# Seven block products of a feed-forward's second matmul in another order, and activation sums, chunks and loads that follow it

## The chip, the cores and the metric

The kernel runs on one core of a Trainium2 chip. The metric is the device time of one execution in microseconds, the median of three runs where nothing else is said. The engines are named as the profile names them: PE (TensorE, matrix products), DVE (VectorE), ACT (ScalarE), POOL (GpSimd) and SP (SyncE, which here issues the loads and stores).

## The reference

A block of two layers works on 1024 latent tokens and 256 context tokens of 1024 features, all in float32. Each layer normalises its input (RMS norm with a scale and a shift made from a conditioning vector), mixes the tokens by attention, adds a gated residual, normalises again and runs a feed-forward; the first layer's attention looks at a neighbourhood of a grid, the second one's at all tokens, with normalised queries and keys. Cut to what matters here:

```python
h_lat = ada_norm(x, g, shift, scale)
x = x + gate1 * mixer(h_lat, h_ctx)
h = ada_norm(x, g2, shift2, scale2)
a, g = split(h @ w_in, 2)           # 1024 -> 2 * 2816
x = x + gate2 * ((silu(g) * a) @ w_out)   # 2816 -> 1024
```

The context's tokens go through the same steps in layer 0 only, and after layer 1 a last norm with a scale and a shift gives the output.

## The kernel before, in words

Every product of float32 numbers is made of three products of shorter words: an operand is split into a high word (a cast, on ACT) and a low word (operand minus high word, `combine` on DVE, L951, or POOL, L948), and PE multiplies high by high, high by low and low by high. So each weight and each activation costs one cast and one subtraction beside its matmuls.

The two feed-forwards (`class Ffn`, one object for each layer) use seven block products in place of eight. The latent tokens form two blocks of 512 (block 0 and block 1), and `PARTS` names the products P1 to P7: each has a weight, plain (W11, W12, W22) or a sum (S1 to S4), and an activation, plain (A11, A21, A22) or a sum (T1 to T4). In the first matmul (`mm1`, L1443 to L1445) the outer loop runs over `NJ` = 22 chunks of 128 hidden features, and each chunk goes through its products. The first `fill` chunks do only P1 and P2 at first (in layer 0 with the context's part, C22 and C21); the rest of their products follows in a second pass. `load1` loads each chunk's raw weights into the cells of the stock `raws`, `feed1` starts an `operand` for each split (L1419), `sums` makes the activation sums T1 to T4 for each quarter k. In the second matmul (`mm2`, L1684 to L1686) the outer loop runs over the products in the order of `ORDER2`; each takes four PSUM banks and 11 steps of three matmuls into each bank, 132 matmuls. `load_t` and `load_w` load its activations and weights, `feed2`, `weight2` and `value2` split them. `drain` then empties the banks: it adds a bank to the residual rows of those quadrants that `SUMS2` names (`add`, L1726), and one partial product, U2, is kept in SBUF, completed by a second product and added to three quadrants from there, 12 additions of 128x512. `load_c` loads the residual rows that these additions go to. In layer 0 the context's second matmul follows (`ctx2`, L1339 to L1341, four quarters), fed by `feed_ctx`. At its start, `load_h` loads the first block's residual rows for the norm, and `ctx_norm` the context's.

`norm` (L121) squares eight rows of a block on ACT (L156), adds them on DVE and POOL (L144), lets PE sum over the partitions (L189) and takes the root on ACT; `apply_norm` scales the rows and splits them (L210, L134, L198, L131, L132). After the first feed-forward `norms1` runs it for both blocks for layer 1, whose key and value projections come next; after the second one `finals` and `output` run the last norm and store the result.

The order on every engine is fixed beforehand: `Lanes` (`bg`) is a planner that runs all these generators against modelled costs, in three lines of priority (`bg.enter(tag, generator, delay, line)`, line 0 first), and writes each instruction to the program where its generator gets the engine. On the chip each engine then goes through its list strictly in order, and waits where an operand isn't there. A changed delay, line or order therefore moves instructions of all engines.

## Time and profile before

| | us |
|---|---|
| median of 3 runs (lowest, highest) | 3114.68 (3112.24, 3115.24) |
| the profiled execution's own time | 3110.32 |
| its span from first to last instruction | 3108.5 |
| PE busy | 2941.1 (95%) |
| DVE busy | 2321.2 (75%) |
| POOL busy | 1800.0 (58%) |
| ACT busy | 1619.0 (52%) |
| chain of work that ended last, by engine | PE 68%, DVE 10%, POOL 6%, DMA 6% |

The mean granted clock of TensorE is 0.985 of full speed. The first feed-forward lies between about 750 and 1700 us, the second from about 2380 to the end; the attention of layer 1 lies between them. The profile is one execution, the median is over three others.

### The profile page before, as it was taken

Reading aid. Unit: us, or ns where it says so; the run is one execution under the profiler, and the core shown is the slowest. Engines: PE = TensorE matmul, PEld = TensorE weight load, DVE = VectorE, ACT = ScalarE, POOL = GpSimd, SP = SyncE. Lnnn points to the kernel's source line nnn. Section 1 sums busy time; section 2 is a strip of 40 time slices with the busy share of each in tenths; the row PEclk is TensorE's granted clock in tenths of the full one; section 3 lists DMA queues with packets and bytes.
Section 4 is the critical chain, followed back from the end, with each engine's and each line's share of the span. In section 5 each row is a group of like instructions: output and inputs, shape, how many; then the busy total and the mean of one; then the engine's idle time right before and its main releaser. Section 6 shows DMA issues by size and latency. Waiting matters only on the chain.

```text
span 3108.5 us, 50198 instructions
## 1 busy us (share of the span) xinstructions
PE 2941.1 (95%) x16460; PEld 2512.9 (81%) x16460; DVE 2321.2 (75%) x4287; ACT 1619.0 (52%) x3735; POOL 1800.0 (58%) x1484
## 2 busy tenths in 40 slices
PE   7999998998899999999988899999999899999997
PEld 4898997887688888887868778888887678888885
DVE  7488778775887677556797588899897786666668
ACT  4345546775642322234455488898886623333444
POOL 4246556765675454346786156666644685445676
PEclk9999999999999999999999999999999999999999
DMA  7777767787335554258455523333323343234862
GB/s 260 216 239 235 231 216 224 235 229 219 132 122 178 169 180 159 77 200 288 164 181 195 166 83 99 98 102 106 106 76 119 125 142 105 102 108 166 314 196 87
DMA packets 306019, 516.94 MB, mean 166 GB/s; under 512 B 46304, under 2 KB 111968, under 8 KB 303968
## 3 DMA queue, kind: packets, MB, share of 16 engines
q1 hardware_dynamic: 305760, 513.74, 51.1%
q8 instruction: 131, 2.15, 0.3%
q14 instruction: 128, 1.05, 0.1%
HBM read 387.52 MB, written 120.18 MB: 163 GB/s over the span
## 4 chain that ended last, share of the span: by engine, by line
PE 68%; DVE 10%; POOL 6%; DMA 6%; issue 4%; ACT 4%; SPq 1%; DVEq 0%; POOLq 0%; ACTq 0%
PE pf L1445 9%; PE pf L1443 9%; PE pf L1444 9%; PE T L863 5%; PE o L494 5%; PE ps L766 3%; PE ps L767 3%; PE ps L768 3%; PE pf L1686 2%; PE pf L1685 2%; PE pf L1684 2%; PE S L2220 2%; PE S L2221 2%; POOL c L948 1%; DMA K<-Kd 1%
## 5 line engine op out<-in xcount | busy, mean ns | idle before, releaser
L856 POOL TENSOR_SCALAR Pt<-Pt,rc 128x1280 f32<-128x1280 f32 (+3 forms) x288 | 298.4, 1036 | 391.5 <-ACT pT L871 139.6
L871 ACT CAST pT<-T 128x256 fp32r<-128x256 f32 (+2 forms) x672 | 304.8, 477 | 122.8 <-PE T L863 118.4
L876 DVE TENSOR_TENSOR pT<-T,pT 128x256 fp32r<-128x256 f32 (+2 forms) x672 | 342.1, 535 | 31.3 <-ACT pT L871 30.9
L863 PE MATMUL T<-ident,Pt 128*128 128x128 f32 x1952 | 303.2, 275 | 22.6 <-POOL Pt L856 22.0
L863 PEld LDWEIGHTS T<-ident,Pt 128*128 128x128 f32 x1952 | 235.5, 141 | 78.6 <-POOL Pt L856 34.7
L494 PE MATMUL o<-pT,Vt 128*128 128x256 f32 x1952 | 296.0, 290 | 2.3 <-DVE pT L876 2.2
L766 PE MATMUL ps<-ah,wh 128*128 128x512 f32 (+1 forms) x688 | 261.2, 380 | 5.2 <-ACT ah L429 2.3
L494 PEld LDWEIGHTS o<-pT,Vt 128*128 128x128 f32 x1952 | 254.8, 189 | 9.5 <-DVE pT L876 5.6
L767 PE MATMUL ps<-al,wh 128*128 128x512 f32 (+1 forms) x688 | 251.3, 365 | 5.3 <-POOL al L132 3.6
L768 PE MATMUL ps<-ah,wl 128*128 128x512 f32 (+1 forms) x688 | 251.0, 365 | 1.4 <-DVE wl L335 1.4
L845 ACT ACTIVATE Pt<-S,rc 128x512 f32<-128x512 f32 (+2 forms) x384 | 247.2, 654 | 9.7 <-DVE rc L837 6.2
L948 POOL TENSOR_TENSOR c<-c,c 128x512 fp32r<-128x512 f32 (+1 forms) x104 | 152.7, 1471 | 125.9 <-ACT c L1419 85.9
L1445 PE MATMUL pf<-ah,wl 128*128 128x512 f32 x480 | 190.4, 397 | 17.6 <-DVE wl L951 15.6
L2212 DVE TENSOR_REDUCE nm<-S 128x1 f32<-128x512 f32 x256 | 169.7, 683 | 35.3 <-PE S L2221 33.6
L1443 PE MATMUL pf<-ah,wh 128*128 128x512 f32 x480 | 190.0, 396 | 2.2 <-ACT wh L1419 2.2
L1444 PE MATMUL pf<-al,wh 128*128 128x512 f32 x480 | 189.4, 395 | 0.0
L891 POOL TENSOR_TENSOR r<-ob 128x256 f32<-128x256 f32 x144 | 123.5, 857 | 65.2 <-ACT ob L885 59.1
L845 ACT ACTIVATE Pt<-X,rc 128x256 f32<-128x256 f32 x256 | 125.1, 489 | 64.9 <-DVE rc L837 58.1
L1419 ACT CAST wh<-c 128x512 fp32r<-128x512 f32 x111 | 68.7, 620 | 169.1 <-POOL c L948 60.1
L768 PEld LDWEIGHTS ps<-ah,wl 128*128 128x128 f32 x688 | 130.9, 190 | 23.2 <-DVE wl L335 2.1
L767 PEld LDWEIGHTS ps<-al,wh 128*128 128x128 f32 x688 | 131.9, 192 | 18.4 <-POOL al L132 5.3
L766 PEld LDWEIGHTS ps<-ah,wh 128*128 128x128 f32 x688 | 131.5, 191 | 18.3 <-ACT ah L429 2.5
(598 smaller groups left out, 9530.5 us busy)
## 6 DMA issues: line engine op xcount, KB each, us to landing
wr<-in_wqkv SPq DMA_DIRECT2D x53, 512.0 KB, 4.5
rope<-in_fout SPq DMA_DIRECT2D x98, 256.0 KB, 3.8
wr<-in_adaT SPq DMA_DIRECT2D x96, 256.0 KB, 3.0
c<-in_fout SPq DMA_DIRECT2D x77, 256.0 KB, 3.5
rope<-in_fin SPq DMA_DIRECT2D x69, 256.0 KB, 3.0
adaw<-in_adaT SPq DMA_DIRECT2D x64, 256.0 KB, 3.7
wr<-in_wo SPq DMA_DIRECT2D x32, 512.0 KB, 4.0
K<-Kd SPq DMA_DIRECT2D x64, 224.0 KB, 4.4
```

Of the source, the lines that this page charges most:

```text
L494: t.matmul(o_ap, lhsT=u.V[:, kb, :], rhs=u.pT[:, i, :], start=i == 0, stop=i == len(u.blocks) - 1)
L766: t.matmul(ps, lhsT=hi[:, c], rhs=ah[:, kc, :n], start=kc == 0, stop=False)
L767: t.matmul(ps, lhsT=hi[:, c], rhs=al[:, kc, :n], start=False, stop=False)
L768: t.matmul(ps, lhsT=lo[:, c], rhs=ah[:, kc, :n], start=False, stop=kc == KC - 1)
L845: s.activation(u.Pt[:, off:off + u.wid[c]], u.S[c], AF.Exp, bias=u.min, scale=u.sign, accum_out=u.rc[:, 3 + c:4 + c])
L856: g.tensor_scalar(Pt, Pt, u.rc[:, 2:3], 1.0, ALU.mult, ALU.mult)
L863: t.transpose(T[:, i * P:(i + 1) * P], u.Pt[:, (i0 + i) * P:(i0 + i + 1) * P], ident[:])
L871: s.copy(u.pT[:, i0:i0 + n, :P], u.T[c])
L876: v.tensor_tensor(u.pT[:, i0:i0 + n, P:], u.T[c], u.pT[:, i0:i0 + n, :P].bitcast(F32), ALU.subtract)
L1443: t.matmul(ps[:], lhsT=r32(hi[:, c]), rhs=bh, start=k == 0, stop=False)
L1444: t.matmul(ps[:], lhsT=r32(hi[:, c]), rhs=bl, start=False, stop=False)
L1445: t.matmul(ps[:], lhsT=r32(lo[:, c]), rhs=bh, start=False, stop=k == 3)
```

## The change

The second matmul's products go P7, P1, P6, P3, P2, P5, P4 in place of P7, P6, P4, P1, P2, P5, P3: a product with a weight sum (P7, P6, P3, P5) is now mostly followed by one with a plain weight (P1, P2, P4), P6 and P3 alone stand next to each other. U2 now starts with P1 and is completed by P6; its 12 additions enter the planner one by one on the last line. Block 1's quadrants end with P5, the sixth, and block 0's with P4, the seventh, so `norms1` and `finals` take block 1 first, and the activation cells of block 1 in place of block 0 become free first. `fill` grows from 4 to 5 chunks in layer 0 and from 7 to 9 in layer 1, the first two chunks' second pass has P4 last, and the splits of these chunks go on line 0. `sums` makes all four T3, then all T2, then all T1, then T4, where each quarter went through its sums by itself, and the split of A22 moves from first to last. The cells are shared out in another way (layer 0 starts with two raw cells in place of four, layer 1 has ten in place of twelve in its main part). `load_h` issues a row each 1000 ns of the plan, the context's rows wait for its end, `load_c` sleeps 1800 ns of the plan between rows, and the context's splits go on line 0. In all the program has 8 more DMAs (256 KB each), one more instruction on ACT, one on POOL and four on DVE; PE's number stays.

```diff
-            added.append(bg.now + 600 + 700 * i)
-            yield from bg.sleep(600 + 700 * i)
+            spent = max(600 + 700 * i, bg.cost)
+            added.append(bg.now + spent)
+            yield from bg.sleep(spent)
...
-    ORDER2 = "P7", "P6", "P4", "P1", "P2", "P5", "P3"
+    ORDER2 = "P7", "P1", "P6", "P3", "P2", "P5", "P4"
...
-            self.fill = fill = (4, 7)[layer]
+            self.fill = fill = (5, 9)[layer]
...
-                    self.todo.append((j, parts[2:], False))
+                    self.todo.append((j, ["P7", "P6", "P5", "P3", "P4"] if j < 2 else parts[2:], False))
...
-            self.raws, self.ring, self.S = Stock(raws), Stock(), Stock(fresh(own))
-            self.outs = Stock(outs if self.layer else [])
+            self.raws, self.ring, self.S = Stock(raws), Stock(), Stock()
+            self.outs = Stock(outs + fresh(own) if self.layer else self.raws.idle[2:])
+            if self.layer == 0:
+                del self.raws.idle[2:]
...
+            all_ = lambda x: [(x, i, "f") for i in range(4)]
...
-            bg.enter(self.tag, self.split(a22, *self.ops["A22", k], ("A22", k)), 0.0, self.line)
...
-            yield "DG0"
-            combine(a12, a12, a11, ALU.subtract)
-            bg.enter(self.tag, self.split(a12, *self.ops["T1", k], ("T1", k)), 900.0, self.line)
-            yield from self.said(("T3", k))
+            yield from self.said(("T3", k), *all_("T3"))
...
+            self.mark(("T2", k, "f"))
...
-            yield from self.said(("T2", k), ("T1", k), ("A22", k))
+            yield from self.said(*all_("T2"))
+            yield "DG"
+            combine(a12, a12, a11, ALU.subtract)
+            self.mark(("T1", k, "f"))
+            yield from self.said(("T2", k), *all_("T1"))
...
+            bg.enter(self.tag, self.split(a12, *self.ops["T1", k], ("T1", k)), 900.0, self.line)
+            bg.enter(self.tag, self.split(a22, *self.ops["A22", k], ("A22", k)), 900.0, self.line)
+            yield from self.said(("T1", k), ("A22", k))
...
-            bg.enter(self.tag, self.split(f, *self.ops["T4", k], ("T4", k)), 900.0, self.line)
+            bg.enter(self.tag, self.split(f, *self.ops["T4", k], ("T4", k)), 0.0, self.line)
...
-                self.raws.idle += self.xrs
+                self.raws.idle += self.xrs + self.tmp[3:]
...
-                self.outs.idle += self.Tf + self.tmp[3:]
+                self.outs.idle += self.Tf
...
-                self.raws.idle += self.tmp[:4]
-                self.outs.idle += self.Tf + self.tmp[4:] + self.xrs
+                self.raws.idle += self.xrs
+                self.S.idle += self.Tf
+                self.outs.idle += self.tmp
...
-            self.ring.idle += fresh(self.sp + self.tempp, F32R)
+            while len(self.temps.idle) < 4:
+                yield ""
+            self.ring.idle += fresh(self.sp[:3] + self.tempp, F32R)
...
-                bg.enter(self.tag, self.ctx_split(u, self.uraw.pop(u), hi, lo), 0.0, 1)
+                bg.enter(self.tag, self.ctx_split(u, self.uraw.pop(u), hi, lo), 0.0, 0)
...
+            yield from self.said("h")
...
-                    bg.enter(self.tag, self.operand(j, x, raw, left, uses[x], sums, hi, lo), 0.0, 1)
+                    bg.enter(self.tag, self.operand(j, x, raw, left, uses[x], sums, hi, lo), 0.0, 0 if i < self.fill else 1)
...
-                self.acells0 = new(0)
-                self.traw.idle += self.acells0
+                self.traw.idle += new(0)
...
-                self.traw.idle[:0] = cells[NP:]
+                self.acells1 = cells[NP:]
+                self.traw.idle[:0] = self.acells1
...
+                self.mark((j, "c22"))
...
+                yield from self.known((j, "c22"))
...
-                if x == "P5" and self.layer == 0:
-                    self.traw.leave(self.acells0, lambda: self.when.update({"act 0": bg.now}))
+                if x == "P4" and self.layer == 0:
+                    self.traw.leave(self.acells1, lambda: self.when.update({"act 1": bg.now}))
...
-                    if name == "P6":
+                    if name == "P1":
...
-                        yield from self.known(("u", "P6", m))
+                        yield from self.known(("u", "P1", m))
...
-            if name == "P1":
-                yield from self.known(("u", "P1", m))
+            if name == "P6":
+                yield from self.known(("u", "P6", m))
...
-                    yield from self.add(x, m, self.U2[m])
+                    bg.enter(self.tag, self.add(x, m, self.U2[m]), 0.0, 2)
...
+                    yield from bg.sleep(1800)
...
-            ffn0.at[0, kc] = bg.now + 3500
-            yield from bg.sleep(CFG["lh"])
+            ffn0.at[0, kc] = bg.now + 6000
+            yield from bg.sleep(1000)
+        ffn0.when["h"] = bg.now
...
-        while not all((0, kc) in ffn0.end for kc in range(KC)):
+        while not all((1, kc) in ffn0.end for kc in range(KC)):
...
-        for b in range(2):
+        for b in (1, 0):
...
-        while b == 0 and "act 0" not in ffn0.when:
+        while b and "act 1" not in ffn0.when:
...
-        while not all((0, kc) in ffn1.end for kc in range(KC)):
+        while not all((1, kc) in ffn1.end for kc in range(KC)):
...
-        for b in range(2):
+        for b in (1, 0):
...
-                                   lambda rs, b=b: output(b, rs), 2 * b, 0))
+                                   lambda rs, b=b: output(b, rs), 2 - 2 * b, 0))
...
```

How instructions move, at three places. Rows are as the program has them; line numbers of the changed kernel are up to 16 higher.

SP, the loads at the start of the first feed-forward, before (`c` from `H0d_122` are the first block's residual rows, `xn` and `sq` from `H0d_124` the context's):

```order
645 L81 DMA c_10505<-H0d_122 128x512
646 L81 DMA xn<-H0d_124 128x256 x4
647 L81 DMA sq<-H0d_124 128x256 x4
648 L81 DMA c_10506<-H0d_122 128x512
649 L81 DMA c_10507<-H0d_122 128x512
650 L81 DMA c_10508<-H0d_122 128x512
651 L81 DMA wr<-in_wo 128x1024
```

and with the change:

```order
645 L81 DMA c_10505<-H0d_122 128x512
646 L81 DMA c_10506<-H0d_122 128x512
647 L81 DMA wr<-in_wo 128x1024
648 L81 DMA c_10507<-H0d_122 128x512
649 L81 DMA c_10508<-H0d_122 128x512
650 L81 DMA c_10509<-H0d_122 128x512
651 L81 DMA c_10510<-H0d_122 128x512
652 L81 DMA c_10549<-in_x 128x512
```

The seven later rows of the block come ahead of the context's eight, where these stood between the first row and the second; the rows for weights or stores between them are left to the gaps in their numbers.

DVE, the drains of the product that completes U2, before (`pf` is a PSUM bank, `c_15258` to `c_15261` are U2, L1726 is `add`):

```order
2289 L951 TENSOR_TENSOR c_15258<-c_15258,pf_10558 128x512
2290 L1726 SCALAR_TENSOR_TENSOR c_15315<-pf_10558,modB_84,c_15315 128x512
2291 L1726 SCALAR_TENSOR_TENSOR c_15307<-c_15258,modB_84,c_15307 128x512
2292 L1726 SCALAR_TENSOR_TENSOR c_15262<-c_15258,modB_84,c_15262 128x512
2293 L1726 SCALAR_TENSOR_TENSOR c_15343<-c_15258,modB_84,c_15343 128x512
2294 L951 TENSOR_TENSOR c_15259<-c_15259,pf_10552 128x512
2295 L1726 SCALAR_TENSOR_TENSOR c_15317<-pf_10552,modB_84,c_15317 128x512
2296 L1726 SCALAR_TENSOR_TENSOR c_15309<-c_15259,modB_84,c_15309 128x512
2297 L1726 SCALAR_TENSOR_TENSOR c_15264<-c_15259,modB_84,c_15264 128x512
2298 L1726 SCALAR_TENSOR_TENSOR c_15345<-c_15259,modB_84,c_15345 128x512
```

and with the change (there `c_15265` to `c_15268` are U2, L1740 is `add`, L952 the split's subtraction):

```order
2278 L952 TENSOR_TENSOR c_15268<-c_15268,pf_10558 128x512
2279 L952 TENSOR_TENSOR ah_15216<-rope,ah_15216 128x512
2280 L1740 SCALAR_TENSOR_TENSOR c_15337<-c_15265,modB_84,c_15337 128x512
2281 L952 TENSOR_TENSOR ah_15216<-c_10549,ah_15216 128x512
2282 L1740 SCALAR_TENSOR_TENSOR c_15269<-c_15265,modB_84,c_15269 128x512
2283 L952 TENSOR_TENSOR al_15279<-ah_15216,al_15279 128x512
2284 L952 TENSOR_TENSOR wl<-al_15179,wh 128x512
2285 L952 TENSOR_TENSOR al_15217<-c_10550,al_15217 128x512
2286 L952 TENSOR_TENSOR c_11552<-ah_15178,c_11551 128x512
2287 L1740 SCALAR_TENSOR_TENSOR c_15489<-c_15265,modB_84,c_15489 128x512
2288 L952 TENSOR_TENSOR c_11556<-ah_15178,c_11555 128x512
2289 L1740 SCALAR_TENSOR_TENSOR c_15357<-c_15266,modB_84,c_15357 128x512
```

The three additions from U2 followed each bank at once; now they stand among the splits of the next products, one or two at a time.

DVE, the end of the context's second matmul, before (L1351 empties its last banks, L144 is the context's norm):

```order
2424 L951 TENSOR_TENSOR c_16810<-rope,c_11456 128x512
2425 L951 TENSOR_TENSOR c_16809<-c_10549,c_16808 128x512
2426 L951 TENSOR_TENSOR c_11459<-rope,c_16806 128x512
2427 L1351 SCALAR_TENSOR_TENSOR c_16729<-pf_10555,modB_84,c_16729 128x256
2428 L1351 SCALAR_TENSOR_TENSOR c_16729<-pf_10553,modB_84,c_16729 128x256
2429 L1351 SCALAR_TENSOR_TENSOR c_16730<-pf_10554,modB_84,c_16730 128x256
2430 L1351 SCALAR_TENSOR_TENSOR c_16730<-pf_10557,modB_84,c_16730 128x256
2431 L144 TENSOR_TENSOR y<-y,sq 128x256 x4
2432 L2092 TENSOR_TENSOR c_17794<-S,c_17794 128x4x64
2433 L144 TENSOR_TENSOR y<-y,sq 128x256 x2
```

and with the change (L1363 empties the banks, L211 and L134 are `apply_norm` of block 0):

```order
2426 L952 TENSOR_TENSOR c_11549<-c_10548,c_16791 128x512
2427 L952 TENSOR_TENSOR c_16793<-c_10549,c_11556 128x512
2428 L211 SCALAR_TENSOR_TENSOR xn<-c_15391,G_1_87,rs 128x512
2429 L134 SCALAR_TENSOR_TENSOR al_17347<-xn,modA_83,ah_17346 128x512
2430 L1363 SCALAR_TENSOR_TENSOR c_16669<-pf_10553,modB_84,c_16669 128x256
2431 L1363 SCALAR_TENSOR_TENSOR c_16669<-pf_10551,modB_84,c_16669 128x256
2432 L1363 SCALAR_TENSOR_TENSOR c_16670<-pf_10558,modB_84,c_16670 128x256
2433 L1363 SCALAR_TENSOR_TENSOR c_16670<-pf_10556,modB_84,c_16670 128x256
2434 L144 TENSOR_TENSOR y<-y,sq 128x256 x4
2435 L2107 TENSOR_TENSOR c_17802<-S,c_17802 128x4x64
```

The last scaling and the last low word of block 0's norm now stand right ahead of the context's last drains; before, only the context's splits stood there.

## Rows read from the trace of the kernel before

**Rows 1.** The page, busy us of each engine, its share of the span and instructions

```profile
PE 2941.1 (95%) x16460; PEld 2512.9 (81%) x16460; DVE 2321.2 (75%) x4287; ACT 1619.0 (52%) x3735; POOL 1800.0 (58%) x1484
```

**Rows 2.** Slices: length, busy PE, PEld, DVE, ACT, POOL, granted clock, DMA share, GB/s

```profile
750.00:800.00 50.00, 36.09 (x147) 26.69 (x146) 20.69 (x28) 18.45 (x36) 15.79 (x14) 0.83 0.64 204
800.00:850.00 50.00, 44.89 (x238) 37.62 (x236) 44.32 (x50) 36.35 (x67) 34.16 (x23) 1.00 0.38 128
850.00:900.00 50.00, 45.52 (x229) 38.60 (x230) 45.89 (x42) 22.56 (x41) 43.00 (x28) 0.93 0.30 103
1400.00:1450.00 50.00, 42.85 (x180) 34.95 (x179) 36.20 (x35) 19.86 (x36) 33.37 (x22) 0.93 0.86 296
1450.00:1500.00 50.00, 50.00 (x222) 41.44 (x221) 19.89 (x23) 22.84 (x41) 29.06 (x22) 1.00 0.58 191
1541.50:1698.50 157.00, 137.45 (x798) 119.66 (x797) 135.94 (x117) 84.24 (x147) 126.83 (x83) 0.95 0.62 202
1600.00:1650.00 50.00, 44.38 (x246) 39.32 (x247) 48.48 (x38) 25.56 (x44) 44.78 (x29) 0.88 0.55 180
1650.00:1700.00 50.00, 46.10 (x368) 44.60 (x368) 34.08 (x37) 27.22 (x48) 30.09 (x21) 1.00 0.67 219
2450.00:2500.00 50.00, 38.36 (x147) 28.88 (x146) 43.38 (x38) 25.61 (x46) 43.81 (x29) 0.93 0.20 68
2850.00:2900.00 50.00, 49.38 (x218) 40.35 (x217) 37.75 (x34) 19.64 (x32) 33.92 (x21) 1.00 0.88 319
3000.00:3050.00 50.00, 47.12 (x205) 38.05 (x204) 48.68 (x37) 26.39 (x47) 47.97 (x31) 1.00 0.57 184
3050.00:3100.00 50.00, 41.17 (x166) 30.23 (x164) 41.11 (x38) 21.33 (x37) 32.79 (x22) 1.00 0.10 38
```

**Rows 3.** PE's waits, 750 to 900 us: waiter, waited for, total, times, longest

```profile
PE pf L766 <- ACT wh L678: 8.5, 1, 8.5
PE pf L1445 <- DVE wl L951: 8.1, 3, 4.6
PE pf L189 <- DVE c L144: 5.6, 3, 3.6
```

**Rows 4.** Timeline of ACT, 766 to 776 us: start, length, instruction, idle before

```profile
773.28 2.01 ACT L156 ACTIVATE c<-c 128x512 f32<-128x512 f32 x3 [4.04 <-DMA c<-H0d]
775.20 0.60 ACT L678 CAST wh<-wr 128x512 fp32r<-128x512 f32 x1
```

**Rows 5.** Timeline of SP's DMA issues, 762 to 772 us

```profile
763.39 2.08 SPq L81 DMA_DIRECT2D xn<-H0d  x4
766.47 2.40 SPq L81 DMA_DIRECT2D sq<-H0d  x4
```

**Rows 6.** PE's waits, 1400 to 1450 us

```profile
PE pf L1685 <- POOL c L948: 7.2, 1, 7.2
```

**Rows 7.** Timeline of POOL, 1398 to 1418 us

```profile
1414.09 1.26 POOL L948 TENSOR_TENSOR ah<-rope,ah 128x512 f32<-128x512 f32 x1 [10.37 <-DMA rope<-in_fout]
```

**Rows 8.** PE's waits, 1541 to 1700 us

```profile
PE pf L189 <- DVE y L144: 5.5, 2, 4.2
...
PE pf L1340 <- DVE c L951: 3.1, 1, 3.1
PE pf L1341 <- DVE c L951: 3.0, 4, 1.2
```

**Rows 9.** Timeline of DVE, 1505 to 1533 us

```profile
1510.13 0.68 DVE L951 TENSOR_TENSOR c<-c,pf 128x512 f32<-128x512 f32 x1
...
1515.02 0.74 DVE L1726 SCALAR_TENSOR_TENSOR c<-pf,modB,c 128x512 f32<-128x512 f32 x1
1515.68 5.18 DVE L1726 SCALAR_TENSOR_TENSOR c<-c,modB,c 128x512 f32<-128x512 f32 x3
```

**Rows 10.** PE's waits, 2380 to 2500 us

```profile
PE pf L1445 <- DVE wl L951: 7.5, 4, 3.3
```

**Rows 11.** PE's waits, 2985 to 3108 us

```profile
PE pf L189 <- DVE o L144: 3.9, 2, 2.9
```

More of the change, by code (lines that the diff above doesn't have):

```diff
@@ L1125, in start_norms @@
         def start_norms(self):
-            tmp = Temps(**dict(zip(("nacc", "nacb"), ([c] for c in self.tmp))), nsq=self.tmp[2:4], nrs=self.tmp[4:5])
+            tmp = self.ntmp = Temps(**dict(zip(("nacc", "nacb"), ([c] for c in self.tmp))), nsq=self.tmp[2:4], nrs=self.tmp[4:5])
             for b in range(2):
@@ L2493, in output @@
         for k0 in range(0, KC, 2):
-            bg.enter("final", scale(k0, k0 == 4 or b == 0), 0.0, 1)
+            bg.enter("final", scale(k0, k0 == 4 or b == 1), 0.0, 1)
         while left:
```

## Prediction

> **What bounds the kernel now.** I read the page's busy shares first, then the table of slices, then TensorE's waits slice by slice, and last the timelines of the engines it waited for. TensorE is busy in 2941 of 3108.5 us [rows 1], so at most 167 us can be won without removing matmuls, and the change removes none (16344 in the program before and after; only their places differ). The slices show where the change can reach [rows 2]. TensorE's 50 us are full between the feed-forwards' ends. They are not full in five places, all inside or beside the two feed-forwards, and in each of them the change moves something: the start of the first one (750 to 900 us, 23.5 us idle), the step from its first to its second matmul (1400 to 1450, 7.2 idle), its end with the context's part (1541.5 to 1698.5), the start of the second one (2450 to 2500, 11.6 idle) and its end (3000 to 3100, 11.7 idle). In four of the five, VectorE and GpSimd are both at 65 to 97% of the slice: the splits of each operand into two words, the sums and the norms run on those two, and TensorE waits for them. The fifth, at 1400, moves 296 GB/s and its DMA engines are 86% busy: there loads are the limit.
>
> The profiled execution took 3110.3 us, 4.4 less than the median of the runs, 3114.7. The sum below is made against 3110.3, and 4.4 are added at its end. A difference of 0.2% is 6.2 us; less than that a measurement of this kernel can't tell from no change.
>
> **Start of the first feed-forward.** TensorE waits 8.5 us once for the second half of a weight's cast, 5.6 us in three waits for the norms' sums of squares, and 8.1 us in three waits for low words [rows 3]. The 8.5 us come from ScalarE's fixed order: four squares of the norm stand ahead of that cast at 775.20, and the second of them waited 4.04 us for its row of the residual [rows 4]. It came late because the eight context loads, 2.1 and 2.4 us of issuing, stood between the first and second load of the residual on SP [rows 5]. The change moves those eight behind the residual's and spreads the cast between the squares. I keep 1.5 of the 8.5: gain 7. Of the 5.6 the first wait (3.6) loses most of its cause, but block 1's sum now stands ahead of the first product P1, where before one product covered it: I count a gain of 2.5 and a loss of 2.5. The 8.1 arise at the first product with a sum, P7 of chunk 0, which comes 72 matmuls later by the additional chunk, 24 of them whole ones at 50/222 us (the full slice at 1450 [rows 2]) and 48 for the context of half the columns at 0.125 (46.10 us for 368, the slice at 1650), 11 us in all; the four sums of its kind are now all made first. I keep 2: gain 6. The granted clock of 0.83 and 0.93 [rows 2] puts 24 us of these slices at the lower level (1.2 GHz); about half of that was idle, so 12 us did the work of 6; one such piece goes, gain 2. Against it stand eight more loads, one more cast and its low word, and three or four more VectorE operations on loaded engines: 3 us at 0.75 us for each operation. **14 us**, between 6 (only the first wait goes) and 22 (all idle time but 1.5 goes).
>
> **Step to the second matmul.** TensorE waits 7.2 us for a split on GpSimd [rows 6]: on GpSimd the sum of P6's first weight, which waited 10.37 us for its load, stands ahead of it [rows 7]. With P1 second, which needs no sum, this sum moves away. The residual's 16 loads of 0.26 MB each, 4.2 MB where the slice at 1400 moves 14.8, no longer follow one another without a pause: they come 1.8 us apart and leave room. But 18 loads of activation sums now stand on SP ahead of P1's first weight, so a new wait there is likely. The clock's 0.93 costs at most 3.5 us. Bounds: a gain of 8 (all but 2.7 of the 10.7) and a loss of 4 (a wait of the old size at the second product, with some of the old one left). **2 us**, near the middle, since the queue is full either way.
>
> **End of the first feed-forward.** A product has 132 matmuls, at 50/222 us 29.7 us; the context's part has 528 of half the columns at 0.125 us, 66 us. Two products and the context would be 125.4 us; they took 157.0 [rows 2], so 31.6 are lost. Waits for a norm's sum are 5.5 of it and waits for the context's low words on VectorE 6.1 [rows 8]; the rest are other waits and a clock of 0.95. In the order of the program, VectorE and GpSimd have 194 operations from the drains of the fifth product to the context's end, and 189 with the change. In the slice at 1600, where both are full, 67 operations took 50 us, 0.746 each. So 189 take 141 us, and that, not 125.4, is the earliest end: gain 16. Inside it the norm comes 85 matmuls after P5's end and not in the next product's first bank, so its 5.5 us go. Block 0's norm now ends with the context, whose successor, the key and value projections, begins with block 0; the 141 contain that wait. Of the twelve additions from SBUF, up to 1.73 us each [rows 9], none is in this stage, before or after. I take 3 off for pieces where the two engines wait themselves. **13 us**, between 5 (only the five operations, 3.7, and one wait) and 24 (the 31.6 without the context's waits).
>
> **Second feed-forward.** Start: 11.6 us idle, 7.5 of waits around low words [rows 10], and a clock of 0.93 that costs up to 3.5: 15 at most. Two more chunks without sums put 48 matmuls, 10.8 us, ahead of the first sum. **12 us**, between 5 and 15. Step to its second matmul: 0.6 us idle in the slice at 2850, though DMA is 88% busy there; ten cells for raw weights in place of twelve may bring half of the 7.2 us of the first. **-1 us**, between -4 and 1. End: 11.7 us idle in the two slices, a part of it after the last matmul; the waits for a norm's sum are 3.9 [rows 11]. The last product, P4 in place of P3, needs no weight sum, and block 1's norm runs in its course. **5 us**, between 2 and 9.
>
> The sum is 14 + 2 + 13 + 12 - 1 + 5 = 45 us: 3110.3 - 45 = 3065.3, and with the 4.4 3069.7 for the median: **3070 us**. The terms lie in different stages, and their ends don't fall together; squares of the half widths add up to about 16, so the forecast's own range is 3048 to 3090.
>
> **Rivals.** *Half of it.* The two elementwise engines keep what they have to do: priorities shift waits and don't remove them, and each term comes to its lower end or little above: 6 - 1 + 5 + 6 - 1 + 3 = 18, 3097 in all. For it: VectorE and GpSimd are at 96% and 90% in the slice at 1600 and the counts hardly change. Against it: before 1541 (the slice at 1450 has them at 40 and 58%) there is room to which work is moved.
>
> *Dearer pairs: slower.* An addition on VectorE with its inputs in SBUF takes 1.73 us beside GpSimd, where one with an input from PSUM takes 0.68 or 0.74 [rows 9]. With the change these additions stand among the splits and no longer in a block of their own, and sums of one kind come at once. If by that an operation costs 0.865 us (half of 1.73, GpSimd doing one in the same time) wherever the two engines are the bound, the end of the first feed-forward takes 189 x 0.865 = 163.5 us, 6.5 more than now; its start, where 143 operations took 100 us, 24 more, of which the added chunk covers about 6; the start of the second, with 67 in 50 us, 8 more, taken from its gain. In place of 14, 13 and 12 stand -18, -6 and 4: 45 - 59 = -14, and with the 4.4 3129 us. It decides from about 0.83 us for an operation on, between 0.72 and 0.865 in the ratio of 45 to 14. Against it: the slices at 800 to 900 and at 1600 are at 0.70 and 0.75 with the same kinds of operations, and the change adds five in all. The Trainium skill, SBUF — State Buffer, "Who interferes with whom", says that a VectorE instruction with two SBUF inputs and a GpSimd instruction that reads SBUF contend for a read port, and that whoever comes second there stands still for the whole of the other's instruction. By that rule a pair would cost the sum of both alone, an estimate of 0.68 + 1.26 us from these rows, and 189 operations 183 us if all were such pairs; the trace agrees in direction, and in size its 1.73 stays below 1.94.
>
> *Late loads.* SP issues in order. If the 18 loads ahead of P1's weight, or the residual's rows at 1.8 us (16 of them take 29 us, and the first drains come 29.7 us after the first product's start), are late, TensorE waits at the second product in both feed-forwards as long as now at the first, 7.2 and 3.5 for the clock: 2 and -1 become -9 and -11. 45 - 21 = 24, and 3091 us. For it: 296 and 319 GB/s in these slices. Against it: a whole product lies between.
>
> **How the numbers follow.** Forecast 0.62, half of it 0.18 (0.05 of that within 0.2%), late loads 0.08, dearer pairs 0.12 (0.02 within 0.2%). Faster 0.62 + 0.13 + 0.08 = 0.83, within 0.2% 0.07, slower 0.10. The range goes from 3046, the forecast's own lower end and a little, to 3112, which takes in both smaller gains and leaves out most of the slower case.
>
> **What would show it.** Right: no wait of ScalarE for the residual's second row near 768 us; TensorE idle under 10 us between 750 and 900; the sixth and seventh product under 32 us each; the stage from the sixth product to the key projections' start 138 to 148 us, VectorE and GpSimd both over 90% in it; the slice with the second feed-forward's first P7 over 45 us busy. Wrong: operations of 0.80 us and more on the two engines in those stages, a wait for a load at the second product, a wait of more than 20 us ahead of the key projections, or a clock under 0.9 in the context's part.

## The result, and the profile after

The changed kernel takes 3080.63 us, the median of four runs (3075.16 to 3084.33), beside 3113.46 us for the kernel before in the same runs. The ratio is 0.9893 with a 95% interval of 0.9876 to 0.991: about 33 us faster, where 45 were forecast, and inside the forecast's range. The profiled execution took 3080.29 us with a span of 3078.5, 30.0 less than the span before. One run of the experiment with early cells (3616.39 us) and one of that with paced loads (4842.41 us) fell in a slower state of the chip and are left out of the medians below.

The page's first lines of the changed kernel, which answer to [rows 1]:

```profile
span 3078.5 us, 50271 instructions
...
PE 2936.6 (95%) x16460; PEld 2511.9 (82%) x16460; DVE 2339.7 (76%) x4291; ACT 1618.8 (53%) x3736; POOL 1807.9 (59%) x1485
```

The busy times stay what they were but for 18.5 us more on DVE and 7.9 on POOL; what went is mostly PE's idle time, 167 before and 142 now, and 4.5 us of its busy time. Slices of the changed kernel, with the columns of [rows 2]; the fourth is the first two products of layer 0's second matmul, the fifth the stretch from its sixth product to the context's end:

```profile
750.00:800.00 50.00, 43.32 (x184) 33.70 (x183) 27.40 (x31) 22.79 (x43) 22.80 (x19) 0.93 0.67 224
800.00:850.00 50.00, 47.62 (x263) 40.11 (x262) 43.13 (x51) 36.68 (x68) 32.48 (x22) 0.97 0.41 137
850.00:900.00 50.00, 45.69 (x234) 38.78 (x234) 44.34 (x40) 22.41 (x42) 43.60 (x29) 0.93 0.31 103
1371.30:1441.60 70.30, 62.06 (x265) 50.60 (x264) 48.88 (x42) 28.91 (x50) 46.82 (x32) 0.95 0.95 335
1531.40:1676.30 144.90, 132.63 (x801) 115.60 (x800) 120.98 (x110) 81.63 (x141) 114.75 (x76) 1.00 0.62 200
2450.00:2500.00 50.00, 38.81 (x156) 31.03 (x155) 44.00 (x38) 18.81 (x33) 44.05 (x28) 0.86 0.25 85
```

The stretch that took 157.0 us takes 144.9, at a clock of 1.00 in place of 0.95. The slice at 2450 is as empty as before, and its clock is lower. PE's waits tell which terms came and which did not. First 750 to 900 us, then 1390 to 1450, 1531 to 1677 and 2410 to 2500 (waiter, waited for, total, times, longest):

```profile
PE pf L190 <- DVE c L144: 7.5, 3, 4.7
PE pf L1455 <- ACT wh L1431: 3.4, 1, 3.4
...
PE pf L1698 <- ACT wh L1189: 7.7, 1, 7.7
...
PE pf L1353 <- DVE c L952: 6.6, 7, 1.7
PE pf L1353 <- POOL c L949: 2.1, 2, 1.1
PE pf L1352 <- DVE c L952: 1.9, 4, 0.7
PE pf L190 <- DVE y L144: 1.4, 1, 1.4
...
PE pf L1455 <- ACT wh L1431: 9.2, 1, 9.2
PE pf L1457 <- DVE wl L952: 2.0, 1, 2.0
```

The 8.5 us wait of [rows 3] is gone, and the norm's waits there have grown from 5.6 to 7.5. The 7.2 us of [rows 6] have become 7.7 for a cast at the second product. And the 7.5 us of short waits in [rows 10] have become one of 9.2.

A cut at the same matmuls of both programs gives the forecast's terms. Both programs have the same order on PE up to the 4500th matmul of the program (the 4574th matmul record of each trace), late in the projections ahead of the first feed-forward; from there on the starts of the same stages are compared in the two traces:

| stretch | before | after | measured | forecast |
|---|---|---|---|---|
| 4500th matmul to first matmul of chunk 0, layer 0 | 64.8 | 61.2 | -3.6 | |
| first matmul of layer 0 | 562.8 | 556.3 | -6.4 | the two: -14 |
| first two products of its second matmul | 69.4 | 70.3 | +0.9 | -2 |
| sixth and seventh product | 77.3 | 61.8 | -15.5 | |
| the context's part | 80.1 | 83.1 | +3.1 | the two: -13 |
| first matmul of layer 1 | 437.8 | 435.7 | -2.1 | -12 |
| first two products of its second matmul | 61.9 | 64.4 | +2.6 | +1 |
| sixth product to the last matmul | 76.1 | 68.1 | -8.0 | -5 |

What lies between these stretches differs by 0.4 us in sum, the time up to the 4500th matmul by 1.0 and the tail behind the last matmul by 0.3. In all -30.0.

The same cut serves the experiments. The 4500th matmul, ahead of which all these kernels issue the same matmuls, comes between 753.7 and 762.7 us in the profiled executions; the cut takes that out. It doesn't take out everything. Where PE doesn't wait, stages repeat exactly (the third to fifth product of layer 0 took 89.8 us in eleven of the twelve traces). Where it waits, they don't, even with the same instructions on every engine. The stretch up to chunk 0 took 58.6 to 61.6 us in the eight traces whose program is the changed kernel's up to there. The first two products of layer 0 took 70.1 to 72.0 in four such traces. In layer 1 the first matmul took 434.3 to 435.7 and its first two products 64.4 to 66.1 in three. So the first row's -3.6 is near the low end of -3.2 to -6.2, and by these ranges a difference of 1 to 3 us in such a stage, or of about 4 in the sum, isn't to be read as an effect. "Total" below is the time from the 4500th matmul to the end of the last: 2342.1 us before, 2313.4 in the changed kernel.

### The profile page after: what moved, and what is told of

The parts are those of the page before. It is cut to its first block, busy times and chain, and to the rows that moved or that the text cites. A ratio compares the mean times of both kernels' runs of the same rounds, so it can differ in the third digit from the quotient of the medians.

```text
span 3078.5 us, 50271 instructions
## 1 busy us (share of the span) xinstructions
PE 2936.6 (95%) x16460; PEld 2511.9 (82%) x16460; DVE 2339.7 (76%) x4291; ACT 1618.8 (53%) x3736; POOL 1807.9 (59%) x1485
## 3 DMA queue, kind: packets, MB, share of 16 engines
q1 hardware_dynamic: 306912, 515.84, 51.8%
## 4 chain that ended last, share of the span: by engine, by line
PE 75%; DVE 10%; DMA 5%; ACT 3%; POOL 3%; issue 2%; SPq 1%; DVEq 0%; POOLq 0%; ACTq 0%
PE pf L1457 9%; PE pf L1455 9%; PE pf L1456 9%; PE T L864 5%; PE o L495 5%; PE pf L1699 4%; PE pf L1700 4%; PE pf L1698 4%; PE ps L767 3%; PE ps L768 3%; PE ps L769 3%; PE S L2235 2%; DMA K<-Kd 2%; PE S L2236 2%; DVE c L952 1%
## 5 line engine op out<-in xcount | busy, mean ns | idle before, releaser
L872 ACT CAST pT<-T 128x256 fp32r<-128x256 f32 (+2 forms) x672 | 304.7, 477 | 125.4 <-PE T L864 121.2
L949 POOL TENSOR_TENSOR c<-c,c 128x512 fp32r<-128x512 f32 (+1 forms) x120 | 176.0, 1474 | 91.7 <-ACT c L1431 60.0
L2227 DVE TENSOR_REDUCE nm<-S 128x1 f32<-128x512 f32 x256 | 169.6, 682 | 36.4 <-PE S L2236 34.7
L952 DVE TENSOR_TENSOR c<-c,c 128x512 fp32r<-128x512 f32 (+1 forms) x111 | 128.2, 1168 | 42.3 <-ACT c L1431 24.7
L949 POOL TENSOR_TENSOR wl<-c,wh 128x512 fp32r<-128x512 f32 x59 | 81.6, 1385 | 120.3 <-ACT wh L1431 113.5
L1455 PE MATMUL pf<-c,wh 128*128 128x512 f32 x372 | 144.9, 390 | 0.0
```

What stands on the lines that cost most here:

```text
L872: s.copy(u.pT[:, i0:i0 + n, :P], u.T[c])
L1455: t.matmul(ps[:], lhsT=r32(hi[:, c]), rhs=bh, start=k == 0, stop=False)
```

## The experiments

**Cells for the weight sums of layer 1, early.** In the changed kernel the stock for these sums (`S`) begins empty, since its cells went to hold the results of the two additional chunks; it gets four when the last activation sum has been split.

```diff
             yield from self.known(*(("A", b, kc) for b in range(2) for kc in (k, 4 + k)))
+            if k == 3 and self.layer == 1:
+                self.S.idle += self.tmp[:3]
...
-                self.S.idle += self.Tf
-                self.outs.idle += self.tmp
+                self.S.idle += self.Tf[:1]
+                self.outs.idle += self.Tf[1:] + self.tmp[3:]
```

> The changed kernel, but in layer 1 the stock for weight sums gets three of the norm's cells when the activation sums begin, not four cells after the last of them is split (the other cells go where those three went). Theory 'no cell': the 9.2 us wait of TensorE for the cast of chunk 0's first weight sum (at 2459.8 us in the changed kernel) is the wait for a cell; it falls under 3 us, the first matmul of the second feed-forward gets 6 to 9 us shorter, and the whole kernel 6 to 9 us faster than the changed one, about 3073. Rival 'engines full': VectorE and GpSimd have no free time from 2443 to 2475, so the wait only moves to the next products of chunk 0 and 1; waits for splits between 2450 and 2500 stay at 9 us or more in sum and the time within 3 us of the changed kernel's.

The timeline of POOL in the changed kernel shows the cell: five low words of the activation sums end at 2466.6, and the first difference of two weights (`c<-r,r`) begins there, though PE has waited for it since 2459.8:

```profile
2458.19 8.42 POOL L949 TENSOR_TENSOR c<-c,c 128x512 fp32r<-128x512 f32 x5
2466.57 1.70 POOL L949 TENSOR_TENSOR c<-r,r 128x512 f32<-128x512 f32 x1
```

With the early cells, PE's waits from 2415 to 2520 us:

```profile
PE pf L1459 <- POOL wl L949: 3.0, 1, 3.0
PE pf L1459 <- DVE wl L952: 1.6, 1, 1.6
```

The first matmul of layer 1 takes 427.8 us in place of 435.7, 7.9 less, and the longest wait is 3.0. "No cell" holds and "engines full" falls, for that stage. Of the 7.9 the next two products give back 2.9 (67.3 against 64.4; against the 66.1 of another trace only 1.2) and the end 1.6 (69.6 against 68.1). The total is 2310.3, 3.1 less, and the median 3078.68 us (ratio to before 0.9884, 0.9862 to 0.9906), 2.0 less: for the whole kernel the 6 to 9 us of "no cell" didn't come.

**Activation loads at a pace.**

```diff
                     self.when["T", x, i] = bg.now + 3000
+                    yield from bg.sleep(1500)
```

> The changed kernel, but 1.5 us of the plan between the second matmul's activation loads, so that the second product's weights go between them. Theory 'queue': the wait of 7.7 us at the second product's first weight (at 1401.4 us) comes from 18 activation loads that stand ahead of it on SP and land 0.67 us apart; it falls to 0 to 3 us, and the kernel is 5 to 8 us faster than the changed one in layer 0, with up to 2 more in layer 1, about 3073. Rival 'all transfers': the DMA engines are full from 1380 on, whatever the order; another load is late instead (activations of the second product, or the residual's rows), the stretch from the first product's start to the third's stays within 2 us of its 70.3.

The changed kernel's SP queue from 1390 us and, behind it, ACT from 1392:

```profile
1390.72 5.01 SPq L81 DMA_DIRECT2D al<-FA  x10
1395.84 0.36 SPq L81 DMA_DIRECT2D ah<-FA  x1
1396.96 5.09 SPq L81 DMA_DIRECT2D ah<-FT  x7
1402.40 0.33 SPq L81 DMA_DIRECT2D rope<-in_fout  x1
...
1407.86 0.62 ACT L1189 CAST wh<-rope 128x512 fp32r<-128x512 f32 x1 [13.79 <-DMA rope<-in_fout]
```

Eighteen loads of activations stand ahead of `rope<-in_fout`, the second product's first weight. It is issued at 1402.40, and ACT has waited 13.79 us when it casts it. With the pace the first two products of layer 0 take 59.8 us in place of 70.3 and PE has no wait in them:

```profile
1374.20:1434.00 59.80, 59.80 (x265) 49.53 (x264) 46.21 (x43) 29.09 (x50) 46.22 (x32) 1.00 0.96 340
```

The DMA engines are as full as before (0.96 and 340 GB/s, against 0.95 and 335), so it was the order of the loads and not their amount. Layer 1 gains 3.5 in the same place (60.9 against 64.4). Both are more than the 5 to 8 and up to 2 that were expected. Total 2297.3, 16.1 less than the changed kernel; median 3069.18 us, ratio to before 0.9849 (0.9823 to 0.9874).

**The same pace in the kernel before.** The same edit, in the old order of products.

> The kernel before with nothing but the 1.5 us of the plan between the second matmul's activation loads. There TensorE's 7.2 us wait was put down to GpSimd, whose next instruction waited 10.4 us for a weight of the second product, P6. If loads in the wrong order are the cause in either order of the products, the first product of layer 0 (39.5 us) gets 7 to 10 us shorter and the first two of layer 1 (31.0 and 30.9) about 1 each: 8 to 12 us faster than before, about 3103. If it is the weight sum of P6, which needs its turn on GpSimd whatever the loads do, the first product stays over 36 us and the time within 4 us of before.

The first product takes 30.0 us, 9.5 less, and PE has no wait there. The waits of before name POOL for it [rows 6] and POOL's timeline a load [rows 7]. The sum keeps its place on POOL, behind the same operations, but its load is there 8 us earlier and it waits 1.99 us for it, not 10.37:

```profile
1406.57 1.30 POOL L948 TENSOR_TENSOR ah<-rope,ah 128x512 f32<-128x512 f32 x1 [1.99 <-DMA rope<-in_fout]
```

In layer 1 the first product stays at 31.0 us and the second gains 0.8. Later stages give back a little, the total is 2334.2, 7.9 less; median 3105.57 us, ratio 0.9965 (0.9952 to 0.9978).

**The order of the products alone,** in the kernel before.

```diff
-    ORDER2 = "P7", "P6", "P4", "P1", "P2", "P5", "P3"
+    ORDER2 = "P7", "P1", "P6", "P3", "P2", "P5", "P4"
...
-                    if name == "P6":
+                    if name == "P1":
...
-        for b in range(2):
+        for b in (1, 0):
```

(with `drain`, `load_t`, `leave1`, `norms1` and `finals` as in the change)

> The kernel before with only the new order of the second matmul's products and what goes with it (partial sum copied at P1 and completed at P6, its additions on the last line, block 1 first in the norms behind it); chunks, sums, cells and loads as before. Theory 'the order does it': the ends of both feed-forwards gain as in the changed kernel (from the sixth product's start to the context's end 12 us less than before, the sixth and seventh product of the second feed-forward 10 less), the starts gain nothing: 15 to 25 us faster than before, about 3093. Rival 'the cells do it': without the paced residual loads and the shared cells the ends gain under half of that, and the kernel is within 10 us of the one before.

The sixth and seventh product take 62.1 us in place of 77.3, as with the whole change, and layer 1's end 69.7 in place of 76.1. But the context's part takes 90.8 in place of 80.1. PE's waits from 1600 to 1700 us, in that part:

```profile
PE pf L1341 <- DVE c L951: 5.8, 2, 4.8
PE pf L1341 <- POOL c L948: 5.0, 2, 4.4
PE pf L1340 <- POOL c L948: 3.0, 1, 3.0
```

The slice from its sixth product to the context's end:

```profile
1546.36:1699.28 152.92, 135.93 (x802) 121.01 (x800) 115.61 (x112) 83.27 (x145) 110.46 (x75) 0.94 0.58 188
```

So the order wins the sixth and seventh product of both layers, and in layer 0 it hands two thirds of it on to the next stage. DVE and POOL have 187 operations in the slice, where the kernel before has 200 [rows 2], yet it is only about 4 us shorter. Total 2332.4, 9.7 less than before; median 3105.99 us, ratio 0.9975 (0.9963 to 0.9987): 8 us, under the 15 to 25 of "the order does it". That theory came out in layer 1; in layer 0 the end gains 4.4 of the 12 us, which is what the rival said (under half), and the whole lies within the rival's 10 us.

**The context's splits on line 1.**

```diff
-                bg.enter(self.tag, self.ctx_split(u, self.uraw.pop(u), hi, lo), 0.0, 0)
+                bg.enter(self.tag, self.ctx_split(u, self.uraw.pop(u), hi, lo), 0.0, 1)
```

> The changed kernel with the context's splits on line 1 in place of line 0. The order alone gained 15 us on the sixth and seventh product and lost 11 of it in the context's part (105 us from the sixth product's end to the key projections' start became 123, in the changed kernel it is 115). If the priority of the context's splits keeps that gain, the context's four quarters (83.1 us in the changed kernel) take 5 to 10 us longer here and the kernel is slower by as much. Rival: it is the cells and the room for the ring (the wait for four free ones, the smaller pool); then the quarters stay within 2 us.

(The stretches that this text names, from the sixth product's end to the key projections, are 119.5 us before, 123.0 with the order alone and 115.0 in the changed kernel; its 105 is a slip.) The context's part takes 93.6 us, 10.4 more. PE's waits from 1600 to 1695 us, in that part:

```profile
PE pf L1353 <- POOL c L949: 11.0, 3, 8.5
PE pf L1353 <- DVE c L952: 6.0, 2, 3.3
```

And the slice from its sixth product to the context's end:

```profile
1538.96:1694.65 155.69, 135.56 (x802) 121.27 (x800) 113.99 (x114) 83.48 (x145) 105.47 (x73) 0.92 0.58 187
```

DVE and POOL are at 73 and 68% while PE waits for them: not a lack of engine time, but the order of their lists. The granted clock is 0.92 here, 1.00 in the changed kernel's slice. The context's priority is needed to keep the order's gain. Total 2323.9, 10.5 more than the changed kernel; median 3097.83 us, ratio 0.9947 (0.9932 to 0.9962).

**U2's additions on line 1.**

```diff
-                    bg.enter(self.tag, self.add(x, m, self.U2[m]), 0.0, 2)
+                    bg.enter(self.tag, self.add(x, m, self.U2[m]), 0.0, 1)
```

> The changed kernel with the twelve additions from U2 on line 1, not on the last line. If their low priority is what frees the engines for the splits, waits come back in the fourth and fifth product and the sixth (all 29.9 us in the changed kernel), 3 to 8 us in sum in each layer. If there is room for them in the third to fifth product anyway, all products stay within 0.5 us and the span from TensorE's 4500th matmul to its end within 2 us.

The fourth product takes 31.7 us in layer 0 and 36.4 in layer 1, where the changed kernel has 29.9 in both; the others stay. The fourth product of layer 1, in the changed kernel and here:

```profile
2938.99:2968.91 29.92, 29.92 (x133) 24.77 (x132) 29.81 (x23) 12.81 (x22) 26.73 (x17) 1.00 0.49 162
2945.58:2981.98 36.40, 32.80 (x134) 25.55 (x133) 33.73 (x29) 12.87 (x22) 30.86 (x19) 0.95 0.50 154
```

DVE has 29 operations there in place of 23. The low line matters in layer 1 (6.5 us, inside the expected 3 to 8); layer 0's 1.8 us is less than expected. Total 2320.8, 7.4 more; median 3095.39 us, ratio 0.9936 (0.9913 to 0.9958).

**Four and seven chunks first, as before.**

```diff
-            self.fill = fill = (5, 9)[layer]
+            self.fill = fill = (4, 7)[layer]
```

> The changed kernel with 4 and 7 chunks of block 0 first, as before, in place of 5 and 9. If the additional chunks cover what is done meanwhile, each first matmul gets longer by the cover that goes: 11.4 us in layer 0 and 10.8 in layer 1 at most, less what the eight loads and the splits cost: 8 to 20 us slower than the changed kernel, and the waits at the first weight sums grow. If the elementwise engines set the pace there anyway and the added chunk only brings work forward, it stays within 4 us.

The first matmul of layer 0 takes 562.9 us, 6.6 more, and PE waits 11.0 us for the first weight sum in place of 3.4:

```profile
PE pf L1455 <- ACT wh L1431: 11.0, 1, 11.0
```

That of layer 1 takes 441.7, 6.0 more, and 3.9 more than the kernel before with as many chunks, which had cells for the sums (and differs in other ways too). Total 2327.4, 14.0 more; median 3099.15 us, ratio 0.9949 (0.9934 to 0.9964).

**Activation sums by quarter, as before** (`sums` of the kernel before in the changed one).

```diff
-            yield from self.said(("T3", k), *all_("T3"))
+            yield from self.said(("T3", k))
...
-            yield from self.said(*all_("T2"))
+            yield from self.said(("T2", k), ("T1", k), ("A22", k))
```

> The changed kernel with each quarter's activation sums made one after the other, as before. If the order by kind is what lets P7 of chunk 0 start, the first matmul of layer 0 (556.3 us in the changed kernel) gets 3 to 8 us longer, that of layer 1 (435.7) 2 to 6, and the kernel is 5 to 14 us slower. Rival: with four chunks the first matmul took as long with sums by kind (562.9) as before with sums by quarter (562.8), so it is the fifth chunk alone that won; both matmuls stay within 1.5 us and the kernel within 3 us.

557.1 and 433.9 us for the two first matmuls, 0.8 more and 1.8 less; total 2312.4, 1.0 less; median 3081.37 us, ratio 0.9894 (0.9878 to 0.9911). The order by kind wins nothing that can be seen: the rival holds, with layer 1's matmul just outside its 1.5 us.

**The loads of the first norm as close as before.**

```diff
-            ffn0.at[0, kc] = bg.now + 6000
-            yield from bg.sleep(1000)
+            ffn0.at[0, kc] = bg.now + 3500
+            yield from bg.sleep(CFG["lh"])
...
-            yield from self.said("h")
```

> The changed kernel with the first block's residual loads as close as before and the context's eight not held back behind them. Forecast's step: the 8.5 us wait for the second half of a weight's cast returns, and the stretch from TensorE's 4500th matmul to the first matmul of chunk 0 (61.2 us in the changed kernel, 64.8 before) gets 5 to 9 longer; the kernel about 3087. Rival 'given back': the wait returns, but block 1's norm is then ready earlier and its wait of 4.7 us goes, so the stretch stays within 3.5 us of 61.2, as little as the pace has won so far, and the kernel within 4 us of the changed one.

PE's waits from 755 to 830 us:

```profile
PE pf L767 <- ACT wh L679: 6.9, 1, 6.9
PE pf L190 <- DVE c L144: 6.4, 2, 3.4
```

The wait for the cast is back with 6.9 us, and the norm's waits are 6.4 in two, against 7.5 in three with the pace. The stretch up to chunk 0 takes 66.7 us, 5.5 more (5.1 to 8.1 by the eight traces with the pace), inside what the forecast's step expects. The total is 2318.3, 4.9 more. The median, 3094.55 us (ratio 0.9939, 0.9918 to 0.9961), lies 14 above the changed kernel's; where the rest of that arose in those runs, this one trace doesn't show.

**Both mended waits together**, the early cells and the paced loads.

> The changed kernel with both: early cells for the weight sums of layer 1 and 1.5 us of the plan between the second matmul's activation loads. Both mended waits lie in different stages, so by the stage sums of the two runs that had one each (7.9 us in the second feed-forward's first matmul, 14 in the two steps to the second matmul) the span from TensorE's 4500th matmul to its end is 20 to 24 us shorter than in the changed kernel, and the time 3055 to 3064. Rival: the earlier sums of the one take VectorE and GpSimd time that the other's splits need (the one alone lost 1.9 us at the second product), then under 15 us remain and the time is 3066 or more.

Total 2291.6, 21.8 less than the changed kernel, as the stages' sums told: 427.8 us for the first matmul of layer 1, 59.8 and 60.9 for the first two products of the two layers, so that the first two products give back nothing of the cells' gain now; the end takes 69.7 us, as with either mended wait alone, 1.6 more than in the changed kernel. The median is 3064.62 us (3064.11 to 3070.37), just above the 3055 to 3064 expected, ratio to before 0.9843 (0.9828 to 0.9857): faster than both kernels.

Not tried alone were the 1800 ns between the residual rows of the second matmul, the sharing out of the cells in layer 0, the first chunks' splits on line 0 and P4 last in the second pass of the first two chunks.

## Why the prediction was right, and where it was off

- **The bound and the five places** were read rightly: the time went from just those stretches, and all between them moved by 0.4 us in sum. One reading is off: in the slice at 750 VectorE and GpSimd are at 41 and 32% [rows 2], not at 65 to 97%; the long wait there was for a load. And the half widths give 15, while the forecast's own range is 20 to 22 wide on each side; the measured time lies inside the narrower one too.
- **Start of the first feed-forward, 14 forecast, 10.0 measured.** The wait for the cast went with the load order, and comes back without it (6.9 us). But the step "Of the 5.6 the first wait (3.6) loses most of its cause" failed: PE is there 7.3 us earlier and the last addition on DVE only 6.1, so that the longest of these waits is 4.7 in place of 3.6, and all of them 7.5 in place of 5.6. Of the 8.4 us won at the cast, 4.8 are gone again by chunk 0 in this trace; by the other traces of the same program up to there the start wins up to 2.6 more. The first matmul then wins 6.4, the forecast's 6; the fifth chunk accounts for it, since four chunks give 562.9 with sums by kind and 562.8 before. That "the four sums of its kind are now all made first" had no part in it that can be seen.
- **Step to the second matmul, -2 forecast, +0.9 measured.** The rival "late loads" came true in its mechanism: the 18 loads ahead of P1's weight, which the text counted from the order, make a wait of 7.7 us. It took the old wait's place, so the term stayed near zero. The step that failed is "With P1 second, which needs no sum, this sum moves away": it took the sum in [rows 7] for the cause and not the load that the sum waited for; the kernel before with paced loads, where the sum keeps its place and the wait is gone, shows that it was the load.
- **End of the first feed-forward, 13 forecast, 12.4 measured.** The size came out, but by another way than the forecast's. The products won 15.5 and the context's part lost 3.1. "So 189 take 141 us, and that, not 125.4, is the earliest end" made the two elementwise engines' operations the limit, five fewer at a faster pace (0.746 us each). Measured are 14 fewer (200 before, 186 now) at the pace of before (0.785 and 0.78). The work went to the third to fifth product, where PE never waits and DVE's busy time grew from 51.8 to 80.5 us (two rows below, before and after), as the forecast's argument against "half of it" had it. But the count isn't the limit either: 187 operations took 152.9 us with the order alone and 155.7 with the context on line 1, and the engines are busy at 83 and 79% of the stretch, not over 90%. What counts there is which operation stands first, and that the forecast didn't cost. That 13 and 12.4 are so near is in part luck.

```profile
1451.77:1541.53 89.76, 89.76 (x397) 74.35 (x396) 51.79 (x52) 37.74 (x67) 60.89 (x43) 1.00 0.51 172
1441.63:1531.39 89.76, 89.76 (x398) 74.35 (x396) 80.52 (x72) 38.80 (x68) 65.79 (x43) 1.00 0.58 193
```

- **Start of the second feed-forward, 12 forecast, 2.1 measured.** This is the step that made most of the miss. "Two more chunks without sums put 48 matmuls, 10.8 us, ahead of the first sum" costed the chunks' cover and not their cells: the diff showed that the stock for weight sums begins empty, and the sum was costed as if it could be made at any time. Given cells, the term is 10.0 (437.8 to 427.8), of which the next products give a part back. By chunks and cells (the first differs from the others in more than these): 437.8 with seven and cells (the kernel before), 441.7 with seven and none, 435.7 with nine and none, 427.8 with nine and cells.
- **Step to its second matmul, +1 forecast, +2.6 measured**, for the cause of layer 0: 3.5 of it goes with the pace. **End, 5 forecast, 8.0 measured**, mis-sized on the cautious side: the sixth and seventh product were 11 us over twice 29.9 before, and are 1.6 over now.
- **Half of it:** the measured 30 lie between its 18 and the forecast's 45, but not by its mechanism in the changed kernel, where the sixth and seventh products' waits are gone and 12.4 of their 15.5 us stayed won; with the order alone they did shift, 10.7 of 15.2. **Dearer pairs** is refuted: its 0.83 us for an operation wasn't reached in the stretch to the context's end, and there an operation keeps DVE busy for 1.10 us and POOL for 1.51, before for 1.16 and 1.53. They did get dearer in the third to fifth product, 1.12 us on DVE for 1.00 before, where PE doesn't wait. The twelve additions do stand singly among the splits now and take 1.78 us beside GpSimd, as this row of DVE's timeline in the changed kernel's fourth product has it; on the last line they fall where PE doesn't wait.

```profile
1474.21 1.78 DVE L1740 SCALAR_TENSOR_TENSOR c<-c,modB,c 128x512 f32<-128x512 f32 x1
```

- **The signs named:** the two products and the 138 to 148 us came, and ScalarE waits 0.18 us for the residual's second row in place of 4.04 (the row below); "TensorE idle under 10 us between 750 and 900" (13.4), "both over 90% in it" and "over 45 us busy" did not, and "a wait for a load at the second product", a sign against, came.

```profile
766.82 0.63 ACT L157 ACTIVATE c<-c 128x512 f32<-128x512 f32 x1 [0.18 <-DMA c<-H0d]
```

## What to carry to other kernels

Where a planner deals out buffers, cost a moved step's buffer before its cover: a stock that begins empty is a wait, whatever work is put ahead. When PE waits for an engine that itself waited for a load, look at what that queue issued before it; spacing loads that weren't needed yet gave 14 us in two steps, half as much as the whole change, with the DMA engines just as full. And when a stage's waits vanish, look one stage on: the order of products alone won 15 us and lost 11 right behind it, until the next stage's splits were put first. Counting operations and taking the fullest slice's pace for the limit gave a good number here for a wrong reason.

## What the runs showed of the chip that was not expected

DVE and POOL at 73 and 68% held PE back more than the same two at 83 and 79%, with nearly the same number of operations (187 and 186): a busy share says nothing of which instruction is first in a list. The granted clock was lower where PE waited longer: 1.00 in the stretch of 144.9 us, whose longest wait is 1.7, and 0.92 in the one of 155.7 with a wait of 8.5. And the same program doesn't repeat exactly: the 4500th matmul came between 753.7 and 762.7 us, and behind it stages in which PE waits differed by 1 to 3 us with the same instructions on all engines, while stages without a wait repeated within 0.1. Medians of four runs that differ by 5 us were therefore not taken to tell kernels apart.
